# RWKV-7 chain steps in a hybrid decoder layer: first products per head in half-width tiles with one eviction, and the state decayed ahead on GpSimd

## The chip, the cores and the metric

The kernel runs on one core of one Trainium2 chip. The metric is the device time of one execution in microseconds, lower is better. Engine names are those of the profile: PE is TensorE's matmul, PEld its weight load, DVE is VectorE, ACT is ScalarE, POOL is GpSimd, SP is SyncE, which issues most DMAs. Within one engine instructions run in the order in which they were put into its queue.

## The reference, cut to what matters

One layer of a decoder for 512 prompt tokens and 8 short sampled sequences of 8 tokens (576 tokens in all): RMSNorm, one wide projection, two token mixers side by side (a Mamba-2 part and an RWKV-7 part, 16 heads of 64 each), an output projection, a SwiGLU block and a gated per-layer embedding. The change lies in the RWKV-7 part, whose recurrence per token and head is

```python
def step(s, inp):
    r_t, w_t, k_t, v_t, kk_t, a_t = inp
    s_kk = jnp.einsum('bhvk,bhk->bhv', s, kk_t)
    s = (s * w_t[:, :, None, :] - s_kk[..., None] * (kk_t * a_t)[:, :, None, :]
         + v_t[..., None] * k_t[:, :, None, :])
    return s, jnp.einsum('bhvk,bhk->bhv', s, r_t)
```

Everything is computed in float32.

## The kernel before

**Tiling.** The 16 heads are worked in four quarters of four heads: two column groups `jj`, and in each two heads `e`. Head `e` lies in partitions 0 to 63 or 64 to 127, named `H[0]` and `H[1]`. The 576 tokens are nine groups `g` of 64: group 0 holds the sampled tokens, groups 1 to 8 the prompt. The recurrence is evaluated group by group: within a group it is a set of small matrix products with a triangular inverse `TT`, made beforehand by `solve` and `combine` of the quarter; from group to group a state of 64 by 64 per head is carried on.

**One step of the chain** (`core(g)`, then `prompt_state(g)` and `outp(g)`, for g from 1 to 8 in turn, with group 0 put in after group 1) goes through these hops:

1. PE, line 789: for each `jj` one product with 128-column weights `Gt[:, g, jj, 0]` (both heads side by side) and the 128 columns `sv[:, jj, 0]` (state and values of both heads). Of the 2 by 2 blocks of the result the two on the diagonal are used.
2. These blocks are evicted from PSUM into `xs`: the lower partitions by ACT (line 791, recorded under line 93 as `xs<-cx`), the upper ones by DVE (line 792).
3. PE, line 797: the inverse `TT` times `xs`, four products of 64 by 64. Behind them, line 802 begins the outputs.
4. ACT (line 804) and DVE (line 805) evict the negated result into `suv`.
5. PE, line 823: `dw`, what the group adds to the state. PE, line 812, finishes the outputs, and ACT evicts them into `ar`.
6. DVE, lines 827 to 832: four instructions, one per `jj` and head, each old state times its decay `PC` plus `dw`, written into the `suv` tile of the next group (or into `so` after group 8). Hop 1 of the next step reads it.

`bktok` and `vwin` make transposed operands of coming steps; `sampled` handles group 0. The pool tag `suv` has three buffers, `xs` two; PSUM tiles `cx` have two banks.

**What stands around it.** The text calls, for each quarter, the projections that are still missing, `prep`, `start_states`, `gram`, `bonus`, `decayed`, `inverse` and `chain`. But the order of the instructions on each engine is not that of the text: the tile framework plans it while the program is built, from an estimated timeline of all engines (`schedule_with_timeline_sim=True`), so projections and preparation of the next quarter (`lin` products, recorded under lines 221 to 223; their weight splits `whi` on ACT and `wlo` on POOL or DVE, lines 203 and 206; convolutions, line 395; masks of `gram` on POOL, lines 634 and 638; the solve's elimination steps on DVE, lines 674 and 676) lie between the steps of a chain. A few places are fixed by hand: some fillers are issued after marks that `core` leaves (`marks[q, g]`, its last first-product).

Of the kernel before, what the change touches and what calls it, by code (L numbers as in the profile page):

```python
# [8 lines left out]
F32 = mybir.dt.float32  # L9
F32R = mybir.dt.float32r  # L10
AF = mybir.ActivationFunctionType
ALU = mybir.AluOpType
# [4 lines left out]
P = 128  # L17
# [58 lines left out]
def hybrid_step(ctx, tc, A):  # L76
    nc = tc.nc
    V, S, G, T = nc.vector, nc.scalar, nc.gpsimd, nc.tensor
# [9 lines left out]
    def nm(s):  # L88
        uid[0] += 1
        return f"{s}_{uid[0]}"  # L90

    def act(out, in_, func=AF.Copy, scale=1.0, bias=0.0):
        return S.activation(out, in_, func, bias=bias, scale=scale)  # L93

    def root_ready(ins):

        with tc.issue_after(ins.ins):
            t = cp.tile([P, 1], F32, tag="rr", name=nm("rr"), bufs=2)
            act(t[:], eps_t[:, 2:3], AF.Sqrt)
# [7 lines left out]
    def lin_ps(off=224):  # L107
        return lin_bank()[:, off:off + NT]

    def bank(pool, tag, bufs):  # L110
        return pool.tile([P, 512], F32, tag=tag, name=nm(tag), bufs=bufs)
# [138 lines left out]
    sp = mix.enter_context(tc.tile_pool(name="sp", bufs=1, side="right"))  # L250
# [15 lines left out]
    def cx_ps():  # L266
        return bank(sq_, "cx", 2)

    def tr_ps():
        return bank(sq_, "tr", 1)  # L270
# [7 lines left out]
    def cslot(name, shape=None, dt=F32):  # L278
        return sp.tile(shape or [P, NT], dt, tag="cv", name=nm(name), bufs=3)
# [27 lines left out]
    for k in range(KT):  # L307
        sq = (se, sp)[k % 2].tile([P, NT], F32, tag=f"bk{k % 2}", name=nm("sq"), bufs=2)
        e = G if k in SQP else V
# [143 lines left out]
    H = (slice(0, 64), slice(64, 128))  # L453
    jj2 = (0, 1)
# [266 lines left out]
    def load_states(s):  # L721
        t = sp.tile([P, 8, 2, 64], F32, tag="L", name=nm("S0"))
        nc.sync.dma_start(t[:], A["s_wkv"][s.q])
        return t
# [14 lines left out]
    def chain(s):  # L739
        TT = s.TT  # L740
        q, AR, Gt, BK, vv, PC = s.q, s.AR, s.G, s.BK, s.v, s.PC
        SUV = [None] * 9

        def suv(g):
            if SUV[g] is None:
                SUV[g] = sp.tile([P, 2, 2, 2, 64], F32, tag="suv", name=nm("suv"), bufs=3)
            return SUV[g]

        def vput(g, ps, half):
            src = ps[half].rearrange("p (j c) -> p j c", j=2)  # L750
            for e in range(2):
                act(suv(g)[H[1 - e], :, :, e],
                    src[:, :, e * 64:e * 64 + 64].unsqueeze(2).to_broadcast([64, 2, 2, 64]))

        def vwin(g):

            ps = tr_ps()
            a = min(g, 7) * 64
            for jj in jj2:
                T.transpose(ps[:, jj * P:(jj + 1) * P], vv[jj][:, a:a + 128], ident[:])  # L760
            for i in range(g, min(g + 2, 9)):
                vput(i, ps[:, 0:256], H[i - min(g, 7)])

        bkt = {}

        def bktok(g):
            ps = tr_ps()
            for jj in jj2:
                T.transpose(ps[:, jj * P:(jj + 1) * P], BK[jj][:, g].rearrange("p a t -> p (a t)"), ident[:])
            t = sp.tile([P, 2, P], F32, tag="bkt", name=nm("bkt"), bufs=2)  # L770
            act(t[:].rearrange("p a c -> p (a c)"), ps[:, 0:256])
            bkt[g] = t

        outs = {}
        flat = lambda t: t.rearrange("p e t -> p (e t)")

        def pairs(ps):

            return ps[:, 0:256].rearrange("p (j e c) -> p j e c", j=2, e=2)

        def singles(ps):

            return ps[:, 0:128].rearrange("p (j c) -> p j c", j=2)

        def core(g):
            sv = suv(g)
            xw = pairs(cx_ps())
            for jj in jj2:
                marks[q, g] = T.matmul(xw[:, jj], flat(Gt[:, g, jj, 0]), sv[:, jj, 0], start=True, stop=True)
            xs = sp.tile([P, 2, 64], F32, tag="xs", name=nm("xs"), bufs=2)  # L790
            act(xs[H[0]], xw[H[0], :, 0])
            V.tensor_copy(xs[H[1]], xw[H[1], :, 1])
            ups = cx_ps()
            uw = ups[:].rearrange("p (j v) -> p j v", j=8)
            for jj in jj2:
                for e in range(2):
                    T.matmul(uw[H[e], jj, :], TT[H[e], g, jj, :], xs[H[e], jj, :], start=True, stop=True)  # L797
            outs[g] = ow = singles(cx_ps())
            for jj in jj2:
                for e in range(2):  # L800
                    rho = s.Z[H[e], jj, 1, :] if g == 0 else AR[H[e], jj, g]
                    T.matmul(ow[H[e], jj], sv[H[e], jj, 0, e], rho, start=jj == 0, stop=False,
                             skip_group_check=True)
            act(sv[H[0], :, 1, 0], uw[H[0], 0:2, :], scale=-1.0)
            V.tensor_scalar(sv[H[1], :, 1, 1], uw[H[1], 0:2, :], -1.0, None, ALU.mult)

        def outp(g):
            sv = suv(g)
            ow = outs[g]
            for jj in jj2:  # L810
                for e in range(2):
                    T.matmul(ow[H[e], jj], sv[:, jj, 1, e], Gt[:, g, jj, 1, e], start=False, stop=True,
                             skip_group_check=True)
            out = act(AR[:, :, g], ow)
            if q == 3 and g == 8:
                root_ready(out)

        def prompt_state(g):
            sv = suv(g)
            dw = singles(cx_ps())  # L820
            for jj in jj2:
                for e in range(2):
                    T.matmul(dw[H[e], jj], bkt[g][:, jj, e * 64:e * 64 + 64], sv[:, jj, 1, e], start=True, stop=True)
            so = None
            if g == 8:
                so = sp.tile([P, 2, 64], F32, tag="xs", name=nm("so"), bufs=2)
            for jj in jj2:
                for e in range(2):
                    h = H[e]
                    dst = so[h, jj] if g == 8 else suv(g + 1)[h, jj, 0, e]  # L830
                    V.scalar_tensor_tensor(dst, sv[h, jj, 0, e], PC[h, jj, 7 + g:8 + g], dw[h, jj],  # L831
                                           ALU.mult, ALU.add)
            if g == 8:
                nc.sync.dma_start(A["o_wkv_p"][q], so[:])

        def sampled():
            S0 = load_states(s)
            bktok(0)
            core(0)
            outp(0)  # L840
            sv = suv(0)
            for jj in jj2:
                dps = cx_ps()
                ums = [sp.tile([P, 8, 64], F32, tag="gt", name=nm("um"), bufs=2) for _ in range(2)]
                for e, um in enumerate(ums):
                    G.tensor_tensor(um[:], sv[:, jj, 1, e].unsqueeze(1).to_broadcast([P, 8, 64]),
                                    dmb[:].unsqueeze(2).to_broadcast([P, 8, 64]), ALU.mult)
                for e, um in enumerate(ums):
                    T.matmul(dps[H[e], :], bkt[0][:, jj, e * 64:e * 64 + 64], um[:].rearrange("p b v -> p (b v)"),
                             start=True, stop=True)  # L850
                V.tensor_tensor(S0[:, :, jj, :], dps[:].rearrange("p (b v) -> p b v", b=8), S0[:, :, jj, :], ALU.add)
                G.tensor_tensor(S0[:, :, jj, :], S0[:, :, jj, :], PC[:, jj, 0:8].unsqueeze(2).to_broadcast([P, 8, 64]),
                                ALU.mult)
            nc.sync.dma_start(A["o_wkv_s"][q], S0[:])

        for e in range(2):
            G.memset(suv(1)[H[e], :, 0, e], 0.0)
        vwin(0)
        for e in range(2):
            G.tensor_copy(suv(0)[H[e], :, 0, e], ident[H[e], H[e]].unsqueeze(1).to_broadcast([64, 2, 64]))  # L860
        for g in range(1, 9):
            if g == 2:
                vwin(g)
            bktok(g)
            core(g)
            if g % 2 and 1 < g < 8:
                vwin(g + 1)
            prompt_state(g)
            outp(g)
            if g == 1:  # L870
                sampled()

    YR, marks = [], {}
# [382 lines left out]
    for what in SEQ:  # L1256
# [7 lines left out]
        elif what == "y":  # L1264
            for j in range(6):
                t = cslot("yl")
                nc.sync.dma_start(t[:], yr_d[j][:])
                YR.append(split(t[:], xp, ("xhi", "xlo"), [P, NT], lo_eng=G))
        else:
            ps = lin_ps()  # L1270
            linear(YR[0:6], ps)
            t = cslot("pr")
# [21 lines left out]
    for c in range(8):  # L1294
        ps = lin_ps()
# [59 lines left out]
    for f in range(2):  # L1355
        ps = lin_ps()
# [20 lines left out]
    for k in range(4):  # L1377
        xa, xb, t = ft("xa"), ft("xb"), ft("tt")
# [100 lines left out]
    for a, b in ((0, 320), (320, NT)):  # L1479
# [18 lines left out]
        for c in range(8):  # L1498
# [5 lines left out]
            ps = lin_bank()[:, 0:n]  # L1504
# [8 lines left out]
            t = ft("pg")[:, 0:n]  # L1513
# [8 lines left out]
        ps = rstd_by_token(acc, 1.0 / D, 0, n)  # L1522
        rl = ft("rs")[:, 0:n]
        act(rl, ps)
        for c in range(8):
            h = hs[c][:, a:b]
# [146 lines left out]
```

## Time and profile before

| | us |
|---|---|
| median of 3 timed runs | 1347.17 |
| lowest, highest | 1346.14, 1347.79 |
| span of the profiled execution, first to last instruction | 1349.0 |
| first and last chain product of line 789 begin at | 201.3 and 671.4 |

The profile is of one execution on the chip. Its span is 1.8 us above the median of the timed runs. A row of the grouped view gives line, engine, operation, output and inputs, shape and count, then busy microseconds and the mean nanoseconds of one, then the engine's idle time ahead of it and what ended it. A float32 matmul stands as two PE records. The view of waits gives, for a pair of waiting and releasing instruction, total microseconds, times, and the longest. The view of windows gives for each stretch its length, busy time (and instruction count) of PE, PEld, DVE, ACT and POOL, then the clock granted to TensorE (1 is full speed), the DMA share and GB/s. In the timeline a row is start, duration, engine, line, operation, output and inputs, count, and in brackets the idle time before it with its releaser.

### The profile page before, as it was taken

Reading aid. Unit: us, or ns where it says so; the run is one execution under the profiler, and the core shown is the slowest. Engines: PE = TensorE matmul, PEld = TensorE weight load, DVE = VectorE, ACT = ScalarE, POOL = GpSimd, SP = SyncE. Lnnn points to the kernel's source line nnn. Section 1 sums busy time; section 2 is a strip of 40 time slices with the busy share of each in tenths; the row PEclk is TensorE's granted clock in tenths of the full one; section 3 lists DMA queues with packets and bytes.
Section 4 is the critical chain, followed back from the end, with each engine's and each line's share of the span. In section 5 each row is a group of like instructions: output and inputs, shape, how many; then the busy total and the mean of one; then the engine's idle time right before and its main releaser. Section 6 shows DMA issues by size and latency. Waiting matters only on the chain.

```text
span 1349.0 us, 26596 instructions
## 1 busy us (share of the span) xinstructions
PE 1246.8 (92%) x10525; PEld 1150.7 (85%) x10525; DVE 826.0 (61%) x1443; ACT 618.9 (46%) x1256; POOL 625.6 (46%) x597
## 2 busy tenths in 40 slices
PE   6897999999989978899999969989999999999997
PEld 6787897889868957788779859889999999999997
DVE  6648666887687785943466667886553135443454
ACT  6565436534654463343434364464442124433363
POOL 5425413642355154122456645565654336654642
PEclk9897799899979978889989989998999999999998
DMA  5322242234232412262454542222323222314322
GB/s 164 125 68 66 77 117 63 85 103 116 75 99 78 109 41 80 94 214 83 157 176 131 179 125 72 73 93 88 92 88 87 79 86 82 93 59 149 96 89 71
DMA packets 94461, 135.58 MB, mean 100 GB/s; under 512 B 34705, under 2 KB 39057, under 8 KB 94337
## 3 DMA queue, kind: packets, MB, share of 16 engines
q1 hardware_dynamic: 93760, 133.36, 32.4%
q8 instruction: 83, 1.36, 0.4%
q10 hardware_dynamic: 576, 0.52, 0.1%
q14 instruction: 42, 0.34, 0.1%
HBM read 106.10 MB, written 27.75 MB: 99 GB/s over the span
## 4 chain that ended last, share of the span: by engine, by line
PE 63%; DVE 14%; ACT 4%; issue 4%; DMA 3%; POOL 3%; DVEq 0%; SPq 0%; ACTq 0%; POOLq 0%
PE lin L234 21%; PE lin L1403 8%; PE lin L223 6%; PE lin L221 6%; PE lin L222 6%; DVE h L395 2%; PE lin L1508 1%; PE lin L1509 1%; PE lin L1510 1%; DVE tmp L674 1%; DVE wlo L206 1%; DVE Tt L676 1%; PE lin L613 1%; PE cx L797 1%; DVE suv L831 1%
## 5 line engine op out<-in xcount | busy, mean ns | idle before, releaser
L206 POOL TENSOR_TENSOR wlo<-raw,whi 128x512 fp32r<-128x512 f32 (+1 forms) x108 | 146.4, 1356 | 352.5 <-ACT whi L93 269.5
L93 ACT ACTIVATE whi<-raw 128x512 fp32r<-128x512 f32 (+1 forms) x232 | 143.3, 618 | 259.1 <-PE lin L234 126.4
L221 PE MATMUL lin<-xhi,whi 128*128 128x288 f32 (+1 forms) x784 | 243.3, 311 | 2.5 <-ACT whi L93 2.2
L223 PE MATMUL lin<-xhi,wlo 128*128 128x288 f32 (+1 forms) x784 | 241.5, 308 | 2.3 <-POOL wlo L206 2.3
L222 PE MATMUL lin<-xlo,whi 128*128 128x288 f32 (+1 forms) x784 | 241.5, 308 | 0.3 <-POOL xlo L194 0.3
L206 DVE TENSOR_TENSOR wlo<-raw,whi 128x512 fp32r<-128x512 f32 (+1 forms) x124 | 100.9, 814 | 103.2 <-PE lin L234 60.4
L221 PEld LDWEIGHTS lin<-xhi,whi 128*128 128x128 f32 (+1 forms) x784 | 151.0, 193 | 9.3 <-ACT whi L93 2.6
L223 PEld LDWEIGHTS lin<-xhi,wlo 128*128 128x128 f32 (+1 forms) x784 | 150.7, 192 | 6.2 <-POOL wlo L206 2.8
L222 PEld LDWEIGHTS lin<-xlo,whi 128*128 128x128 f32 (+1 forms) x784 | 150.8, 192 | 4.8 <-issue 1.2
L234 PE MATMUL lin<-xhi,whi 128*128 128x288 f32 x384 | 62.3, 297 | 3.2 <-ACT xhi L93 3.0
L234 PE MATMUL lin<-xlo,whi 128*128 128x288 f32 x384 | 60.8, 298 | 0.0
L234 PE MATMUL lin<-xhi,wlo 128*128 128x288 f32 x384 | 59.3, 297 | 0.0
L234 PEld LDWEIGHTS lin<-xhi,whi 128*128 128x128 f32 x384 | 54.6, 189 | 3.8 <-ACT xhi L93 1.7
L234 PEld LDWEIGHTS lin<-xlo,whi 128*128 128x128 f32 x384 | 54.8, 191 | 0.0
L234 PE MATMUL lin<-ah,wlo 128*128 128x288 f32 x352 | 54.7, 296 | 0.0
L234 PE MATMUL lin<-al,whi 128*128 128x288 f32 x352 | 54.7, 296 | 0.0
L234 PE MATMUL lin<-ah,whi 128*128 128x288 f32 x352 | 54.7, 296 | 0.0
L234 PEld LDWEIGHTS lin<-xhi,wlo 128*128 128x128 f32 x384 | 54.3, 191 | 0.0
L1403 PE MATMUL lin<-T,wh 128*128 128x288 f32 x320 | 50.1, 296 | 4.5 <-DVE T L194 2.8
L674 DVE TENSOR_TENSOR tmp<-L,Tt 72x30 f32<-72x30 f32 (+14 forms) x120 | 49.2, 410 | 3.2
L234 PEld LDWEIGHTS lin<-ah,whi 128*128 128x128 f32 x352 | 49.6, 189 | 0.0
L234 PEld LDWEIGHTS lin<-ah,wlo 128*128 128x128 f32 x352 | 49.6, 189 | 0.0
(425 smaller groups left out, 3197.8 us busy)
## 6 DMA issues: line engine op xcount, KB each, us to landing
raw<-wts SPq DMA_DIRECT2D x271, 256.0 KB, 2.6
S<-s_wkv SPq DMA_DIRECT2D x8, 512.0 KB, 5.1
hd<-s_ssm SPq DMA_DIRECT2D x8, 512.0 KB, 4.5
o_ssm_s<-hd SPq DMA_DIRECT2D x8, 512.0 KB, 2.9
xbc_d<-E SPq DMA_DIRECT2D x12, 288.0 KB, 2.1
x<-xT SPq DMA_DIRECT2D x8, 288.0 KB
gate_d<-g SPq DMA_DIRECT2D x8, 288.0 KB, 2.5
bv_d<-rw SPq DMA_DIRECT2D x8, 288.0 KB
```

What stands on the lines that cost most here:

```text
L93: return S.activation(out, in_, func, bias=bias, scale=scale)
L206: eng.tensor_tensor(lo[:, 0:n], raw[:, 0:n], hi[:, 0:n].bitcast(F32), ALU.subtract)
L221: T.matmul(ps[:, a:b], whi, xhi[:, a:b], start=first, stop=False)
L222: T.matmul(ps[:, a:b], whi, xlo[:, a:b], start=False, stop=False)
L223: T.matmul(ps[:, a:b], wlo, xhi[:, a:b], start=False, stop=last)
L234: T.matmul(ps[:, a:e], (hi, lo)[p][:, i * P:(i + 1) * P], xs[k + i][q][:, a:e], start=n == k + i == 0, stop=n == 2 and k + i == nk - 1, sk ...
L395: V.scalar_tensor_tensor(h[:], E[:, i:i + 600], w(i), h[:], ALU.mult, ALU.add)
L613: T.matmul(ps[:, c:c + 128].rearrange("p (a t) -> p a t", a=2), s.BK[jj][H[e], g].rearrange("p a t -> p (a t)"), s.G[H[e], g, jj, :, e], s ...
L674: V.tensor_tensor(o, L[:, jx:jx + 1, jx + 1:32].to_broadcast([NB, jx, n]), Tt[:, 0:jx, jx:jx + 1].to_broadcast([NB, jx, n]), ALU.mult)
L676: V.tensor_tensor(Tt[:, 0:jx, jx + 1:32], Tt[:, 0:jx, jx + 1:32], o, ALU.subtract)
L797: T.matmul(uw[H[e], jj, :], TT[H[e], g, jj, :], xs[H[e], jj, :], start=True, stop=True)
L1403: T.matmul(ps, (hi, lo)[p][:, k * P:(k + 1) * P], OPS[n][k][q], start=first and p == q == k == 0, stop=p == 1 and k == 3, skip_group_check ...
```

## The change

Line 789's products are made per head: 64-column weights, 64 moving columns, into the head's half of the partitions, so that only the used blocks are computed, and they lie side by side as one 128 by 128 block. One ACT instruction evicts them. For groups 1 to 8 a new function `decay(g)` multiplies the state at the beginning of the step with its decay on POOL, one instruction per head for both `jj`, into a new tile `kept` of one buffer; the state's update on DVE is then one addition of `kept` and `dw` per head for both `jj`.

```diff
-        def pairs(ps):
-            return ps[:, 0:256].rearrange("p (j e c) -> p j e c", j=2, e=2)
+        kept = {}
+        def decay(g):
+            kept[g] = t = sp.tile([P, 2, 64], F32, tag="kept", name=nm("kept"))
+            for e in range(2):
+                h = H[e]
+                G.tensor_tensor(t[h], suv(g)[h, :, 0, e], PC[h, :, 7 + g].unsqueeze(2).to_broadcast([64, 2, 64]), ALU.mult)
...
         def core(g):
             sv = suv(g)
-            xw = pairs(cx_ps())
+            xw = singles(cx_ps())
             for jj in jj2:
-                marks[q, g] = T.matmul(xw[:, jj], flat(Gt[:, g, jj, 0]), sv[:, jj, 0], start=True, stop=True)
+                for e in range(2):
+                    marks[q, g] = T.matmul(xw[H[e], jj], Gt[:, g, jj, 0, e], sv[:, jj, 0, e], start=True, stop=True)
             xs = sp.tile([P, 2, 64], F32, tag="xs", name=nm("xs"), bufs=2)
-            act(xs[H[0]], xw[H[0], :, 0])
-            V.tensor_copy(xs[H[1]], xw[H[1], :, 1])
+            act(xs[:], xw)
+            if g:
+                decay(g)
...
-            for jj in jj2:
-                for e in range(2):
-                    h = H[e]
-                    dst = so[h, jj] if g == 8 else suv(g + 1)[h, jj, 0, e]
-                    V.scalar_tensor_tensor(dst, sv[h, jj, 0, e], PC[h, jj, 7 + g:8 + g], dw[h, jj],
-                                           ALU.mult, ALU.add)
+            for e in range(2):
+                h = H[e]
+                dst = so[h] if g == 8 else suv(g + 1)[h, :, 0, e]
+                V.tensor_tensor(dst, kept[g][h], dw[h], ALU.add)
```

More of the change, by code (lines that the diff above doesn't have):

```diff
@@ L774, in chain @@
         outs = {}
-        flat = lambda t: t.rearrange("p e t -> p (e t)")
-        def pairs(ps):
-            return ps[:, 0:256].rearrange("p (j e c) -> p j e c", j=2, e=2)
+        kept = {}
[4 more added lines that the diff above has]
+                G.tensor_tensor(t[h], suv(g)[h, :, 0, e], PC[h, :, 7 + g].unsqueeze(2).to_broadcast([64, 2, 64]), ALU.mult)
         def singles(ps):
```

## The prediction

> **What bounds the kernel now.** I read the page first, then the windows over the four chains, the waits in them, and the timeline of one step.
>
> ```profile
> span 1349.0 us, 26596 instructions
> ...
> PE 1246.8 (92%) x10525; PEld 1150.7 (85%) x10525; DVE 826.0 (61%) x1443; ACT 618.9 (46%) x1256; POOL 625.6 (46%) x597
> ...
> PE 63%; DVE 14%; ACT 4%; issue 4%; DMA 3%; POOL 3%; DVEq 0%; SPq 0%; ACTq 0%; POOLq 0%
> ```
>
> PE is busy nearly always and holds 63% of the chain that ended last; DVE holds 14% of it, POOL 3%. An average over the span says little of one stage, so here are the windows of the four quarters' chains.
>
> ```profile
> 195.00:320.00 125.00, 117.38 (x1127) 102.46 (x1121) 95.52 (x200) 62.57 (x140) 55.50 (x71) 0.93 0.29 87
> 320.00:440.00 120.00, 111.45 (x1091) 98.05 (x1089) 88.39 (x174) 63.08 (x144) 51.36 (x60) 0.90 0.32 94
> 440.00:555.00 115.00, 101.88 (x1046) 85.82 (x1044) 85.38 (x191) 54.86 (x126) 39.65 (x45) 0.91 0.29 82
> 555.00:680.00 125.00, 116.22 (x1063) 96.21 (x1062) 61.96 (x151) 53.51 (x122) 38.34 (x38) 0.90 0.44 142
> sum 485.00, PE 446.94 PEld 382.54 DVE 331.25 ACT 234.02 POOL 184.84; mean PE 111.73 PEld 95.63 DVE 82.81 ACT 58.50 POOL 46.21
> ```
>
> PE is idle for 485.0 - 446.9 = 38 us here, and its granted clock is 0.90 to 0.93, so it is not simply full. DVE is busy for 74 to 76% of the first three windows. Whatever the chain gains must come from these 38 us, from the clock, or from DVE's queue. The waits of this stretch (total us, times, longest):
>
> ```profile
> POOL wlo L206 <- ACT whi L93: 139.5, 23, 19.2
> ...
> DVE suv L805 <- ACT suv L93: 13.1, 10, 4.2
> ...
> PE cx L789 <- DVE suv L831: 6.6, 4, 2.9
> PE cx L797 <- DVE xs L792: 6.3, 4, 2.8
> ...
> PEld cx L789 <- DVE suv L831: 3.8, 5, 3.0
> ```
>
> The two longest that PE spends on the chain are just the two DVE hops that the change touches: the copy of line 792 and the update of line 831. One step shows why (timeline, and one stretch's granted clock):
>
> ```profile
> 271.22 1.21 DVE L831 SCALAR_TENSOR_TENSOR suv<-suv,pc,cx 64x64 f32<-64x64 f32 x4
> 274.26 0.61 PE L789 MATMUL cx<-suv,G 128*128 128x128 f32 x4
> 274.91 0.27 ACT L93 ACTIVATE xs<-cx 64x128 f32<-64x128 f32 x1 [3.31 <-PE cx L789]
> 277.85 0.32 PE L797 MATMUL cx<-xs,TT 64*64 64x64 f32 x2
> 280.50 0.29 DVE L792 COPY xs<-cx 64x128 f32<-64x128 f32 x1
> 280.84 0.38 PE L797 MATMUL cx<-xs,TT 64*64 64x64 f32 x5 [2.34 <-DVE xs L792]
> 284.24 1.29 POOL L206 TENSOR_TENSOR wlo<-raw,whi 128x512 fp32r<-128x512 f32 x1 [6.59 <-ACT whi L93]
> 284.30 1.43 DVE L674 TENSOR_TENSOR tmp<-L,Tt 72x184 f32<-72x184 f32 x1
> 285.76 0.36 DVE L676 TENSOR_TENSOR Tt<-Tt,tmp 72x184 f32<-72x184 f32 x1
> 288.18 1.19 DVE L831 SCALAR_TENSOR_TENSOR suv<-suv,pc,cx 64x64 f32<-64x64 f32 x4
> ```
> ```profile
> 282.40:285.40 3.00, 3.00 (x15) 2.85 (x13) 2.83 (x7) 1.78 (x4) 1.16 (x1) 0.51 0.58 170
> ```
>
> ACT has its half of `xs` at 275.18. DVE, in the middle of the next quarter's elimination, copies its half only at 280.50. PE starts the inverse product with one half and then stands 2.34 us for the other. Just behind that idle time the granted clock is 0.51 for 3 us, so the wait is paid once more at 3.0 x 0.49 = 1.5 us.
>
> **The change part by part.** Durations of what goes and what comes, and the nearest rows for what the trace has not:
>
> ```profile
> L831 DVE SCALAR_TENSOR_TENSOR suv<-suv,pc,cx 64x64 f32<-64x64 f32 x112 | 31.3, 280 | 13.7 <-PE cx L823 11.2
> L792 DVE COPY xs<-cx 64x128 f32<-64x128 f32 x36 | 10.6, 294 | 15.4 <-ACT xs L93 14.8
> L831 DVE SCALAR_TENSOR_TENSOR so<-suv,pc,cx 64x64 f32<-64x64 f32 x16 | 4.5, 280 | 0.9 <-PE cx L823 0.6
> L623 DVE TENSOR_TENSOR Lst<-lin,dgmask 64x128 f32<-64x128 f32 x8 | 2.3, 288 | 0.8 <-ACT G L93 0.7
> ```
> ```profile
> L93 ACT ACTIVATE ar<-cx 128x128 f32<-128x128 f32 x36 | 9.9, 276 | 17.7 <-PE cx L812 17.4
> L93 ACT ACTIVATE xs<-cx 64x128 f32<-64x128 f32 x36 | 9.6, 268 | 24.8 <-PE cx L789 24.5
> ```
> ```profile
> L638 POOL TENSOR_TENSOR G<-G,gmask 64x256 f32<-64x256 f32 x32 | 21.4, 667 | 10.5 <-ACT G L93 8.6
> ...
> L638 POOL TENSOR_TENSOR G<-G,dgmask 64x128 f32<-64x128 f32 x8 | 3.5, 433 | 4.4 <-ACT G L93 4.1
> ...
> L857 POOL MEMSET suv<- 64x128 f32 x8 | 1.6, 201 | 13.9 <-ACT whi L93 7.7 <-DVE suv L831 6.0
> ```
>
> *One eviction.* ACT's grows from 268 to about 276 ns (a 128x128 PSUM block, as the outputs): nothing. DVE loses 36 x 294 = 10.6 us. PE's wait for it, 6.3 us, goes; what is late next is ACT's eviction, which PE waits for anyway. **-6.3 us.** Two of the waits were over 2 us (2.34 and 2.8), long enough for the slow clock: **-3 us**.
>
> *State update.* Four instructions of 280 ns (1.19 us in the step shown) become two of 64x128 with one PSUM input, 288 ns each by the mask row: 0.6 us, so 0.54 us earlier. PE waited for it nine times (6.6 us in 4, 3.8 in 5); each of them shortens by 0.54: **-4.9 us.** The rest of these waits is DVE's queue and stays.
>
> *DVE's load.* Gone: 10.6 + 31.3 + 4.5 = 46.4 us; added: 64 x 288 ns = 18.4 us; net 28.0 us less. DVE stands in the last chain for 14% of the span and is busy for 61%: 0.23 of an average DVE microsecond is paid for. 28.0 x 0.23 = 6.4, of which 4.9 is counted: **-1.5 us**. The bounds are 0 and, where DVE alone set the end, -28.
>
> *POOL.* Two multiplies per step, 64 in all. The trace has none of them; a 64x128 memset (201 ns) bounds one below and a 64x256 mask product (667) above; I take the 64x128 mask product, 433: 64 x 0.433 = 27.7 us. By POOL's share of the chain (3% against 46% busy) that costs 27.7 x 0.065 = **+1.8 us**. Queued behind each pair are `wlo` (PE waits for that), the masks of `gram` and the products `um`; each may come up to 0.87 us later.
>
> POOL's work is not free for DVE either: the elimination product of 72x184 took 1.43 us at 284.30, while `wlo` ran on POOL until 285.53, and the following one of the same size took 0.36. If each of the 64 multiplies met such an instruction, DVE would lose 27.7 us; with DVE busy 68% of the stretch (331 of 485) and a meeting half over on the average I take 27.7 x 0.68 x 0.5 = 9.4 us, at 0.23: **+2.2 us**. The Trainium skill, "SBUF — State Buffer", section "Who interferes with whom", gives a rule that speaks against the change: a VectorE instruction with two SBUF inputs and a GpSimd instruction that reads SBUF exclude each other for a whole instruction. By it, with every multiply meeting one, this term would be 27.7 x 0.23 = 6.4, and the time 4 us longer than my sum; the 1.43 us above agrees with the rule. The new addition on DVE has one SBUF input, and the old one had one too.
>
> *PE.* Between fillers the new shape is no gain:
>
> ```profile
> 286.18 0.29 PE L221 MATMUL lin<-xhi,whi 128*128 128x288 f32 x1
> 286.40 0.45 PE L823 MATMUL cx<-suv,bkt 128*64 128x64 f32 x8
> 286.68 0.40 PE L812 MATMUL cx<-G,suv 128*64 128x64 f32 x6
> 287.02 0.40 PE L222 MATMUL lin<-xlo,whi 128*128 128x288 f32 x1
> ...
> 290.18 0.29 PE L221 MATMUL lin<-xhi,whi 128*128 128x288 f32 x1
> 290.31 0.61 PE L789 MATMUL cx<-suv,G 128*128 128x128 f32 x4
> 290.67 0.38 PE L222 MATMUL lin<-xlo,whi 128*128 128x288 f32 x1
> ```
>
> From filler to filler the old four records take 290.67 - 290.18 = 0.49 us. Half-width products start 0.22 us after a filler, and 14 of them are 0.62 us up to the next; at that rate 8 take 0.22 + 8/14 x 0.62 = 0.57 us: +0.08 a step, or +3 us in 36 steps. Against it, the inverse product is no longer entered twice (277.85 and 280.84 in the step shown); each such second entry costs 0.22 - 0.13 = 0.09 us of changing shape, in 36 steps at most 3 us. I take **0**, with bounds of 3 us to both sides.
>
> **Sum:** -6.3 - 3 - 4.9 - 1.5 + 1.8 + 2.2 = -11.7 us. Against the profiled span that is 1349.0 - 11.7 = 1337.3; the runs' median, 1347.2, lies 1.8 us under the span, so I predict 1335.5, rounded to **1336 us**, 0.8% faster. No DMA is added or moved, and SP's queue is untouched. The planned order of 485 us is made anew from other costs, which no row prices; I allow 7 us to each side for it.
>
> **The rivals.**
>
> *Late multiplies (slower).* The addition on DVE now also waits for POOL. POOL runs in order, and for 139.5 of these 485 us it stands in front of a `wlo` whose `whi` ACT has not made; the mean wait is 6.1 us, the longest 19.2. A multiply queued behind one comes when that wait and 1.3 us of `wlo` are over. The addition then stands on DVE with the elimination, masks and `wlo` behind it, and the next first product with it. Against it: in the step shown the old state is written at 271.22 + 1.21 = 272.43 and the update that needs the product of POOL comes at 288.18, and 36 steps in 485 us are 13.5 us apart on average, so on average only a wait of more than 13.5 - 1.3 - 0.9 = 11.3 us comes through. A late step costs between 0 and 19.2 - 11.3 = 7.9 us, 4 in the middle, plus 1.5 of slow clock: 5.5. Two of them take 11 us of the 11.7, three make it slower, and five, 27.5 us, give 1347.2 - 11.7 + 27.5 = **1363**. Chance 0.20, milder cases included.
>
> *The wait moves on (no change).* Both hops are followed by another DVE eviction of the same step, line 805, waiting 13.1 us already. If DVE's queue, not the number of hops, sets the pace, the 6.3 and 3 us come back there: -11.7 + 9.3 = -2.4, **1345**. For it: the copy at 280.50 was late for its place in the queue, and line 805 has the same queue. Against it: a hop less is a queueing less. Chance 0.15.
>
> *DVE was the bound (more).* If the first three windows hang on DVE, all its 28 us count, less the 9.4 it loses to POOL: 18.6, and with PE's wait and clock 28: **1320**. For it: 75% busy there, with the elimination in one dependent row. Against it: PE is busy 89 to 94%. Chance 0.13.
>
> That the change does not do what it says would need a second eviction or a fourth update; its text leaves none.
>
> **How the numbers follow.** Forecast 0.52 (1336, own range 1328 to 1343), more 0.13, no change 0.15, slower 0.20. About 0.2%, 2.7 us, is what a measurement of this kernel can tell from no change. Faster by more: 0.52 + 0.13 = 0.65; within: 0.15; slower: 0.20. The range must leave out at most 2 in 10: 1322 leaves out about half of the "more" case, 0.07, and 1353 the worse half of the slower one, 0.11.
>
> **What would show it.** Right: no wait of line 797's product for a DVE copy; the update pair under 0.65 us; DVE's busy time some 20 us lower over the four chains, POOL's 28 higher; the clock there up by 0.01; line 789's last product before 671.4. Wrong: DVE additions that wait for POOL's `kept`; waits of line 805's successors grown by what line 797 lost; first products per head that take longer than 0.6 us from filler to filler; multiplies far from 433 ns; or the time after 680 changed, which none of this touches.

## The result, and the profile after

| | median, us (runs) | ratio to before, 95% interval |
|---|---|---|
| before, run beside it | 1343.52 (20) | 1 |
| after | 1347.51 (20) | **1.0028 [1.0015, 1.0040]** |

The change makes the kernel 0.28% slower: 4.0 us between the medians, where 11.7 us less had been forecast. Ratios leave out the few executions that took far longer: one of before (1392.22 us), and below one of eight of `order_both` (3865.70) and two of twelve of `after_null` (1906.70 and 2253.71). The median of before is itself 3.65 us below that of the three runs shown ahead of the prediction. A second profile of before (below: "before, second profile") has a span of 1340.1 us, 8.9 less than the first, and is the one compared with from here on.

The page of after, and its windows over the four chains (columns as in the prediction):

```profile
span 1348.5 us, 26867 instructions
...
PE 1238.7 (92%) x10669; PEld 1141.4 (85%) x10669; DVE 805.1 (60%) x1343; ACT 617.9 (46%) x1256; POOL 662.3 (49%) x661
...
PE 67%; DVE 13%; ACT 4%; DMA 3%; issue 3%; POOL 2%; SPq 0%; DVEq 0%; POOLq 0%; ACTq 0%
...
L783 POOL TENSOR_TENSOR kept<-suv,pc 64x128 f32<-64x128 f32 x64 | 34.3, 536 | 66.6 <-DVE suv L836 54.5
```
```profile
195.00:320.00 125.00, 115.56 (x1134) 100.61 (x1133) 94.05 (x180) 62.24 (x140) 62.47 (x86) 0.92 0.30 86
320.00:440.00 120.00, 105.80 (x1122) 93.09 (x1121) 81.47 (x150) 63.08 (x145) 60.70 (x76) 0.93 0.31 91
440.00:555.00 115.00, 104.07 (x1046) 87.28 (x1046) 77.83 (x162) 54.05 (x124) 46.72 (x57) 0.82 0.28 80
555.00:680.00 125.00, 114.38 (x1123) 93.37 (x1121) 54.97 (x121) 52.82 (x121) 46.03 (x55) 0.92 0.44 142
sum 485.00, PE 439.81 PEld 374.36 DVE 308.32 ACT 232.18 POOL 215.92; mean PE 109.95 PEld 93.59 DVE 77.08 ACT 58.05 POOL 53.98
```

The third window and the sum of before, second profile:

```profile
440.00:555.00 115.00, 101.06 (x1067) 84.86 (x1065) 88.43 (x199) 56.67 (x130) 40.06 (x45) 0.94 0.30 86
sum 485.00, PE 446.52 PEld 380.71 DVE 331.41 ACT 235.27 POOL 188.85; mean PE 111.63 PEld 95.18 DVE 82.85 ACT 58.82 POOL 47.21
```

The loads moved as the change says: over the four windows DVE has 331.4 - 308.3 = 23.1 us less, POOL 215.92 - 188.85 = 27.1 more. But the third window's clock is 0.82 (0.94 in the second profile of before, 0.91 in the first). PE's groups on the chain's hops between 195 and 690 us show where it stands now. Each row ends with PE's idle time ahead of the group and what ended it; first before (second profile), then after:

```profile
L789 PE MATMUL cx<-suv,G 128*128 128x128 f32 x144 | 29.2, 320 | 7.3 <-DVE suv L831 6.9 <-DVE S L851 0.3
L812 PE MATMUL cx<-G,suv 128*64 128x64 f32 x288 | 28.1, 242 | 0.8 <-ACT suv L93 0.4 <-DVE suv L805 0.3
L797 PE MATMUL cx<-xs,TT 64*64 64x64 f32 x288 | 25.1, 245 | 9.7 <-DVE xs L792 6.1 <-DVE S L851 1.6 <-ACT xs L93 1.5
L613 PE MATMUL lin<-G,bk 64*128 64x128 f32 x216 | 25.1, 343 | 1.7 <-ACT E L93 1.2 <-ACT G L93 0.4
L823 PE MATMUL cx<-suv,bkt 128*64 128x64 f32 x256 | 16.5, 248 | 1.0 <-DVE suv L805 1.0
```
```profile
L613 PE MATMUL lin<-G,bk 64*128 64x128 f32 x216 | 29.8, 392 | 8.8 <-POOL bk L585 4.8 <-ACT G L93 3.9
L818 PE MATMUL cx<-G,suv 128*64 128x64 f32 x288 | 29.0, 249 | 0.9 <-ACT suv L93 0.9
L794 PE MATMUL cx<-suv,G 128*64 128x64 f32 x288 | 19.7, 254 | 7.8 <-DVE suv L836 7.8
L803 PE MATMUL cx<-xs,TT 64*64 64x64 f32 x288 | 18.8, 246 | 5.0 <-ACT xs L93 4.8
L829 PE MATMUL cx<-suv,bkt 128*64 128x64 f32 x256 | 17.0, 253 | 7.8 <-DVE suv L811 7.8
```

In after, line 794 is the first products, 803 the inverse, 829 `dw`, 811 the DVE eviction into `suv`, 836 the addition, 783 the multiply. The inverse products stand 5.0 us instead of 9.7, since no DVE copy is waited for. But `dw` stands 7.8 instead of 1.0, and line 613, the next quarter's `gram`, 8.8 instead of 1.7. All hops, that is these groups without line 613 (and with 0.5 us of line 808 in after): 18.8 us before, 22.0 after.

By stretches, each from one event's start in the timeline to the next (the solve's first DVE instruction, the chain's first product, the first product behind the chain), and the same for the experiment that decided the case:

| stretch, us | before, first and second profile | after | change in before's order, two profiles |
|---|---|---|---|
| start to the second quarter's solve | 276.2, 273.7 | 276.1 | 274.1, 275.3 |
| to the third's solve | 142.2, 142.1 | 142.6 | 142.3, 142.6 |
| to the fourth's solve | 118.2, 115.1 | 119.0 | 116.4, 114.4 |
| to the last chain's first product | 59.3, 58.9 | 59.6 | 57.0, 57.0 |
| last chain | 79.2, 79.1 | 77.8 | 79.0, 79.0 |
| to the SwiGLU block | 210.8, 211.3 | 212.2 | 207.9, 210.2 |
| to the end | 463.3, 459.8 | 461.2 | 459.4, 460.9 |

Two executions of one program, before, differ by up to 3.5 us in a stretch. A difference of that size between single profiles can't be put down to an edit.

### The profile page after: what moved, and what is told of

The parts are those of the page before. It is cut to its first block, busy times and chain, and to the rows that moved or that the text cites. A ratio compares the mean times of both kernels' runs of the same rounds, so it can differ in the third digit from the quotient of the medians.

```text
span 1348.5 us, 26867 instructions
## 1 busy us (share of the span) xinstructions
PE 1238.7 (92%) x10669; PEld 1141.4 (85%) x10669; DVE 805.1 (60%) x1343; ACT 617.9 (46%) x1256; POOL 662.3 (49%) x661
## 4 chain that ended last, share of the span: by engine, by line
PE 67%; DVE 13%; ACT 4%; DMA 3%; issue 3%; POOL 2%; SPq 0%; DVEq 0%; POOLq 0%; ACTq 0%
PE lin L234 22%; PE lin L1407 8%; PE lin L221 6%; PE lin L223 6%; PE lin L222 6%; PE lin L613 2%; PE lin L1512 1%; PE lin L1514 1%; PE lin L1513 1%; DVE h L395 1%; DVE wlo L206 1%; PE cx L818 1%; PE tr L769 1%; PE cx L803 1%; DMA L<-Ld 1%
## 5 line engine op out<-in xcount | busy, mean ns | idle before, releaser
L783 POOL TENSOR_TENSOR kept<-suv,pc 64x128 f32<-64x128 f32 x64 | 34.3, 536 | 66.6 <-DVE suv L836 54.5
L613 PE MATMUL lin<-G,bk 64*128 64x128 f32 x288 | 39.3, 394 | 15.1 <-POOL bk L585 9.0
```

Source lines behind the costliest of these rows:

```text
L613: T.matmul(ps[:, c:c + 128].rearrange("p (a t) -> p a t", a=2), s.BK[jj][H[e], g].rearrange("p a t -> p (a t)"), s.G[H[e], g, jj, :, e], s ...
L783: G.tensor_tensor(t[h], suv(g)[h, :, 0, e], PC[h, :, 7 + g].unsqueeze(2).to_broadcast([64, 2, 64]), ALU.mult)
```

## The experiments

Three theories stood after the result. **Plan:** the steps are shorter, but every edit makes the planner draw the order of all engines anew, and that gave the gain back. **Path:** the waits that went were not on the path that sets the end. **GpSimd:** the multiplies stand in POOL's queue ahead of the next quarter's preparation.

### Each half alone, the multiplies on DVE, and a reordered text, all under the planner

`a_only` has the half-width products and the one eviction, `b_only` the decay ahead on POOL; `ab_dve` is the whole change with the multiplies on DVE; `null1` is before with two lines swapped:

```diff
-                G.tensor_tensor(t[h], suv(g)[h, :, 0, e], PC[h, :, 7 + g].unsqueeze(2).to_broadcast([64, 2, 64]), ALU.mult)
+                V.tensor_tensor(t[h], suv(g)[h, :, 0, e], PC[h, :, 7 + g].unsqueeze(2).to_broadcast([64, 2, 64]), ALU.mult)
...
+            V.tensor_copy(xs[H[1]], xw[H[1], :, 1])
             act(xs[H[0]], xw[H[0], :, 0])
-            V.tensor_copy(xs[H[1]], xw[H[1], :, 1])
```

> Only the first half of the change: first products per head in half-width tiles and one ACT eviction; the state's update stays four DVE instructions. Theory 'GpSimd' (the multiplies on POOL delay the preparation of the next quarter, and eat what the chain gains): 0.996 to 0.999 of before, DVE busy over the four chains about 10 us less, POOL unchanged. Theory 'shape' (half-width products between 128-wide fillers cost PE more than they save): 1.002 to 1.004. Theory 'plan' (every edit redraws the planned order, and that alone moves the time by some tenths of a per cent): anything from 0.996 to 1.004, unrelated to the other parts.

> Only the second half: the decay multiplied ahead on POOL and one addition per head on DVE; products and evictions of the first hop as before. 'GpSimd': 1.003 to 1.006, POOL 30 us busier over the four chains, PE waits for POOL's bk in the gram products (5 us or more). 'Shape': 0.996 to 0.999. 'Plan': unrelated to the sum of the parts, so that the two halves' ratios need not multiply to 1.0028.

> The whole change with the two multiplies on DVE in place of POOL (DVE then has 64 more instructions of about 0.3 us, 18 us less relief). 'GpSimd': 0.996 to 1.000, clearly under the whole change's 1.0028. 'Shape': still 1.002 to 1.004. 'Plan': anything.

> The kernel before with the same instructions; only the two evictions into xs are written in the other order in the text, DVE's ahead of ACT's, which the planner takes as its cue. 'GpSimd' and 'shape': within 0.998 to 1.002. 'Plan': may differ by more than 0.2% either way though no work differs.

Measured: `a_only` 1.0031 [1.0007, 1.0055], `b_only` 1.0078 [1.0049, 1.0108], `ab_dve` 1.0021 [0.9998, 1.0043], `null1` 1.0116 [1.0093, 1.0139]. The halves, +0.31% and +0.78%, don't add to the whole's +0.28%, and `ab_dve` is not clearly under the whole change. So neither half, nor POOL, explains the whole's time by itself. `null1` turned out to be no pure reordering. Its waits, and those of before (second profile), in 195 to 690 us:

```profile
ACT xs L93 <- DVE xs L791: 33.9, 18, 5.7
```
```profile
DVE xs L792 <- ACT xs L93: 14.8, 12, 3.4
```

The two evictions wait for each other in the order of the text. With DVE's first, ACT waits for DVE's queue, 33.9 us in 18 times. How much of its 1.16% is this wait and how much the plan is not shown.

### The change in before's order

The planned order of each engine in before is written out as a table, and neighbours in it are tied by edges of issue order, which add no wait to the program. Products, eviction and additions take the places of what they replace; only the multiplies on POOL are left to the planner. `order_a` and `order_b` do the same with each half. Without the change this gives before's program again.

```diff
+def pin_order(nc, tc):
...
+    for engine, steps in plan.items():
+        at, prev = 0, None
+        for d in steps:
+            at += d
+            ins = own[engine][at]
+            if prev is not None:
+                tc.add_manual_dep(ins, prev.name, mybir.DependencyInfo(
+                    mybir.DependencyClass.NoSync, mybir.DependencyReason.DATA), reason="pin")
+            prev = ins
...
             hybrid_step(ctx, tc, A)
+            pin_order(nc, tc)
```

> The whole change, but with the planned order of before written out as edges of issue order (no waits): every instruction that both kernels share stands where it stands in before on its engine; the products, the one eviction and the two additions stand in the places of what they replace, the two POOL multiplies go where the planner likes. It takes the redraw of the order out of the comparison. Theory 'plan' (the steps are shorter as forecast, and the redrawn order gives the gain back): clearly faster than before, 1334 to 1340 us. Theory 'path' (the waits that went were not on the path that sets the end, so that another wait takes their place whatever the order): within 2 us of before. Theory 'GpSimd' (the multiplies stand in POOL's queue in front of the next quarter's preparation): slower than before by 2 to 8 us.

> Half-width products and the one eviction alone, in the planned order of before. With its own order this half took 1.0031 of before. Theory 'plan': 0.993 to 0.998 of before, since the DVE copy (6.3 us of PE waits) is gone. Theory 'shape' (narrow products between wide fillers cost PE more than the copy did): 1.001 to 1.004. Theory 'path': 0.999 to 1.001.

> State decayed ahead on POOL alone, in the planned order of before. With its own order this half took 1.0078 of before. Theory 'plan': 0.996 to 1.000 (the update is shorter by 0.57 us in 28 steps, most of it under fillers). Theory 'GpSimd': 1.003 to 1.008, as with its own order. With 'plan' the two halves add to the whole in this order, which they don't with their own orders (0.31 and 0.78 per cent against 0.28).

> The whole change in before's order once more, beside the next two, and to see whether the gain stands on another chip or another call. Theory 'plan': 0.993 to 0.998 of before again. If the first result was chance: 0.999 to 1.002.

| in before's order | median, us | ratio to before, 95% interval |
|---|---|---|
| whole change, `order_both` | 1337.57 | 0.9954 [0.9926, 0.9981] |
| whole change again, `order_both2` | 1339.49 | 0.9968 [0.9942, 0.9993] |
| half A, `order_a` | 1342.27 | 0.9990 [0.9970, 1.0010] |
| half B, `order_b` | 1343.95 | 0.9998 [0.9980, 1.0016] |

Each ratio is to the executions of before run beside it (medians 1342.59 us, for `order_both2` 1343.76), and is not the quotient of the two medians.

The same instructions that are 0.28% slower in their own order are 0.46 and 0.32% faster in before's; the intervals don't overlap. That decides for **plan**: in a fixed order the change is worth 0.46 and 0.32%, 0.39% of 1343.5 = 5.2 us between them, and the redraw costs (1.0028 - 0.9961) x 1343.5 = 9.0 us (9.9 and 8.1 by the two runs). It is also the fastest version of the study, ahead of both kernels. The halves' -0.10 and -0.02% are each compatible with nothing and, within their intervals, with adding up to the whole. PE's hops in `order_both`:

```profile
L818 PE MATMUL cx<-G,suv 128*64 128x64 f32 x288 | 28.1, 243 | 1.0 <-ACT suv L93 0.4 <-DVE suv L811 0.4
L613 PE MATMUL lin<-G,bk 64*128 64x128 f32 x216 | 26.7, 360 | 1.9 <-ACT E L93 1.2 <-ACT G L93 0.3 <-POOL bk L585 0.2
L803 PE MATMUL cx<-xs,TT 64*64 64x64 f32 x288 | 22.7, 244 | 5.3 <-ACT xs L93 4.5 <-ACT TT L93 0.8
L794 PE MATMUL cx<-suv,G 128*64 128x64 f32 x288 | 20.4, 252 | 4.7 <-DVE suv L836 4.0 <-ACT ar L93 0.4 <-DVE S L855 0.3
L829 PE MATMUL cx<-suv,bkt 128*64 128x64 f32 x256 | 16.9, 252 | 2.3 <-DVE suv L811 2.3
```

The hops stand 13.3 us here (14.5 in `order_both2`) against 18.8 before and 22.0 in after, and line 613 only 1.9 (4.4). So with the order held, 4.3 to 5.5 us of hop waiting go, about what the time gains. That the one is the other is not shown. `order_a` has only 14.6 us of hop waiting too, and gains 0.10%; `null1` has 17.9, less than before, and is 1.16% slower.

Nor do the profiles show where the 5.2 us are gained. The last chain ends at 675.0 and 669.0 us in the two profiles of before, at 668.7 and 668.2 in those of `order_both` and `order_both2`. What the redraw costs does show there, as far as single profiles tell: five profiles of changed kernels in the planner's order (after, `a_only`, `ab_dve`, and `after_null` and `after_null2` below) end the last chain at 674.7 to 676.2, `b_only` at 681.0, and seven with the order held in whole or in part (these four runs and the first three under "Which engines") at 666.8 to 670.9.

What the redraw did can be seen at two places. The first is POOL near 250 us. After (timelines of POOL and PE):

```profile
250.45 1.85 POOL L783 TENSOR_TENSOR kept<-suv,pc 64x128 f32<-64x128 f32 x2 [0.40 <-DVE suv L836]
252.36 0.60 POOL L389 COPY cso<-E 128x3 f32<-128x3 f32 x1
252.91 0.83 POOL L388 COPY cso<-E 128x24 f32<-128x24 f32 x1
253.69 3.29 POOL L585 TENSOR_TENSOR bk<-lo,lo 64x576 f32<-64x576 f32 x2
```
```profile
251.49 0.49 PE L613 MATMUL lin<-G,bk 64*128 64x128 f32 x4
255.14 1.22 PE L613 MATMUL lin<-G,bk 64*128 64x128 f32 x4 [2.54 <-POOL bk L585]
```

The multiplies were put ahead of the `bk` products, and PE has no other work there and stands 2.54 us for `bk`. In before's order:

```profile
253.64 3.35 POOL L585 TENSOR_TENSOR bk<-lo,lo 64x576 f32<-64x576 f32 x2
257.06 1.70 POOL L783 TENSOR_TENSOR kept<-suv,pc 64x128 f32<-64x128 f32 x2
```
```profile
254.26 0.80 PE L613 MATMUL lin<-G,bk 64*128 64x128 f32 x4
256.02 1.22 PE L613 MATMUL lin<-G,bk 64*128 64x128 f32 x4
```

Here the multiplies come behind `bk`. `bk` is no earlier, but PE has other products in front of that place and its rows carry no wait: the order of two engines together makes the wait. The multiplies are not needed for it: in `a_only` and `ab_dve`, which have none on POOL, line 613 stands nearly as long, and for POOL's `bk` too (first `a_only`):

```profile
L613 PE MATMUL lin<-G,bk 64*128 64x128 f32 x216 | 30.9, 403 | 6.2 <-ACT G L93 3.4 <-POOL bk L585 2.8
```
```profile
L613 PE MATMUL lin<-G,bk 64*128 64x128 f32 x216 | 27.5, 365 | 7.2 <-POOL bk L585 4.0 <-ACT G L93 3.0
```

The second place is the third quarter's chain. Windows of after, and the same distance behind the solve's start of before (second profile); the number after POOL's is the clock:

```profile
498.70:508.70 10.00, 6.02 (x58) 3.73 (x56) 6.93 (x10) 4.95 (x12) 6.74 (x7) 0.82 0.35 112
508.70:518.70 10.00, 10.00 (x116) 8.29 (x116) 3.29 (x9) 3.21 (x11) 3.64 (x7) 0.50 0.18 54
518.70:528.70 10.00, 10.00 (x97) 8.60 (x96) 3.84 (x10) 3.60 (x11) 3.50 (x8) 0.50 0.01 2
```
```profile
495.80:505.80 10.00, 7.98 (x47) 3.44 (x45) 7.80 (x10) 4.24 (x10) 9.68 (x7) 1.00 0.21 59
505.80:515.80 10.00, 7.21 (x99) 5.77 (x98) 7.10 (x20) 5.27 (x17) 4.71 (x8) 1.00 0.32 108
515.80:525.80 10.00, 9.03 (x158) 7.48 (x155) 5.62 (x15) 3.95 (x12) 4.92 (x7) 1.00 0.15 22
```

In after PE never stands for 20 us, but at half the clock; before it stands a fifth of the time at full clock. `gram`'s products take 445 ns in 508.7 to 528 of after and 287 in 505.8 to 525.8 of before. It is the stretch to the fourth solve, 3.9 us longer than in the second profile of before, but only 0.9 longer than in the first. That the clock made it longer is argued, not shown: no run changed the clock alone.

### How far the order alone moves the time

`null2` is before with its four state updates in the order of heads. `after_null2` and `after_null` are after with the first products, and with the additions, written upper head first:

```diff
-            for jj in jj2:
-                for e in range(2):
+            for e in range(2):
+                for jj in jj2:
                     h = H[e]
...
-                for e in range(2):
+                for e in (1, 0):
                     marks[q, g] = T.matmul(xw[H[e], jj], Gt[:, g, jj, 0, e], sv[:, jj, 0, e], start=True, stop=True)
...
-            for e in range(2):
+            for e in (1, 0):
                 h = H[e]
                 dst = so[h] if g == 8 else suv(g + 1)[h, :, 0, e]
```

> Before, with the four state updates of a step written head by head instead of column group by column group: the same four instructions, the same operands, nothing else. Only the planner's order can differ. Theory 'plan': it moves the time by several tenths of a per cent either way (the swap of the two evictions moved it by 1.16 per cent); without it 0.999 to 1.001.

> The changed kernel with the four first products of a step written upper head first instead of lower head first, under the planner: the same instructions, only the order can differ. Theory 'plan': another draw, anywhere from 0.995 to 1.010 of before, and off the changed kernel's 1.0028 by more than the intervals. If 1.0028 belongs to the change itself: 1.002 to 1.004.

> The changed kernel with the two additions of a step written upper head first, under the planner; few places move (89 lines of PE's order against 792 between the changed kernel's own order and before's). Theory 'plan': near the changed kernel, 1.001 to 1.005 of before, since the order is nearly its own.

Measured: `null2` 1.0017 [0.9997, 1.0036], `after_null2` 1.0022 [1.0002, 1.0041], `after_null` 0.9991 [0.9966, 1.0017]. `null2` is a pure reordering, and its interval takes in no change at all: redrawing before's own instructions moves the time less than I expected. But none of the three orders that the planner made for the changed instructions (1.0028, 1.0022, 0.9991) is as fast by its ratio as before's order (0.9954, 0.9968), and `after_null` and `after_null2` show the same stands on `dw` (7.9 and 6.8 us) and on line 613 (8.3 and 6.2). So the loss is not in one draw alone. It is not equal in all either: `after_null` is no slower than before, and its interval overlaps those of before's order. Three orders are too few to tell how the planner's orders spread.

### Which engines, and POOL once more

`order_pe` holds PE alone to before's order, `order_rest` (with the four other names in the same place) DVE, ACT, POOL and SP; `order_both_dve` holds all, with the multiplies on DVE.

```diff
     for engine, steps in plan.items():
+        if engine not in ('PE',):
+            continue
```

> The whole change with PE's order alone held to that of before; the planner orders DVE, ACT, POOL and SP anew round it. Theory 'plan, on PE' (what the redraw costs is where the fillers stand on PE between the hops): as fast as with all engines held, 0.993 to 0.998. Theory 'plan, on the side engines' (the order of preparation on DVE, POOL and ACT makes the next quarter's solve late): 1.000 to 1.004, as the change with its own order.

> The whole change with DVE, ACT, POOL and SP held to before's order and PE left to the planner. With PE alone held the gain was gone (1.0004), with all held it was there (0.9954, 0.9968). Theory 'side engines': as all held, 0.994 to 0.998. Theory 'both': 0.999 to 1.003.

> The whole change in before's order, with the two multiplies of a step on DVE instead of POOL. Theory 'GpSimd' (head-of-line waiting of the multiplies in POOL's queue costs time): faster than the whole change in that order by 2 us or more. Theory 'POOL is cover': the same within 2 us, or slower by the 64 multiplies that DVE then carries in the solve's stretches.

> Before unchanged, for a profile of an execution near its median: the profiled one lay at 1349.0 us between first and last instruction, with the clock at 0.89 in the first 195 us where every later profile of any kernel has 0.93. Expected: a span of 1338 to 1344 us, the clock at 0.93 there, and the same stages up to that shift.

Measured: `order_pe` 1.0004 [0.9979, 1.0030], `order_rest` 0.9973 [0.9954, 0.9992], `order_both_dve` 0.9987 [0.9962, 1.0013]. The gain survives when the side engines are held and not clearly when PE is; their intervals still overlap, so this points to the side engines and doesn't settle it. Off POOL, the multiplies make nothing faster, as 0.9987 against 0.9954 and 0.9968 shows: **GpSimd** falls as a cause by itself. Where the planner puts the multiplies in POOL's queue, as near 250 us, belongs to the plan. `before_again`, the second profile, ran once, in 1341.79 us, with a span of 1340.1 as expected. Its stages were not the first profile's up to a shift, as expected: the stretch to the fourth solve took 115.1 us against 118.2.

### What a hop is worth

`order_slow` is before, in its order, with one more link in every step:

```diff
             V.tensor_copy(xs[H[1]], xw[H[1], :, 1])
+            xc = sp.tile([P, 2, 64], F32, tag="xc", name=nm("xc"), bufs=2)
+            V.tensor_copy(xc[:], xs[:])
...
-                    T.matmul(uw[H[e], jj, :], TT[H[e], g, jj, :], xs[H[e], jj, :], start=True, stop=True)
+                    T.matmul(uw[H[e], jj, :], TT[H[e], g, jj, :], xc[H[e], jj, :], start=True, stop=True)
```

> Before, in before's order, with one more link in every step: after the two evictions DVE copies xs (128x128) into a second tile, and the inverse products read that one. It prices a hop: 36 links of about 0.4 us each (an estimate from the DVE copy of 64x128, 0.28 us, and the distance between two instructions on DVE). Theory 'cover' (fillers on PE hide a hop but for the few steps where PE stands, as the waits of before show: some ten of 36): 3 to 8 us slower. Theory 'every hop counts': 12 to 18 us slower. Theory 'path' (the chain's hops don't reach the end at all): within 2 us.

Measured: 1.0083 [1.0054, 1.0113], 11.2 us slower, above "cover" and just under "every hop". Its rows of PE and of the copy, 195 to 690 us:

```profile
L799 PE MATMUL cx<-xc,TT 64*64 64x64 f32 x288 | 22.7, 248 | 28.5 <-DVE xc L794 25.1 <-ACT TT L93 3.3
```
```profile
L794 DVE COPY xc<-xs 128x128 f32<-128x128 f32 x36 | 17.1, 476 | 1.2
```

The inverse products stand 28.5 us instead of 9.7, while the first products behind them stand 2.9 instead of 7.3; over all hops it is 33.3 instead of 18.8. So 14.5 us more waiting came with 11.2 us more time (7.3 to 15.2 by the interval), about three quarters. The copy also puts 17.1 us of work on DVE, so not all of it need be the wait. **Path** falls for a longer hop: it does reach the end, and here it shows in the stages too, as the last chain ends at 685.3 us. That a shorter hop pays at the same rate is not shown.

## Why the prediction was wrong

The forecast was 1336 us, 0.8% faster; the time is 1347.5, inside the range and on the other side. Point by point:

**The step that failed is the last of the sum: "The planned order of 485 us is made anew from other costs, which no row prices; I allow 7 us to each side for it."** It was given no sign and stood outside the sum, as if the two sides were equally likely. It cost 9.0 us, more than the rest was worth, and none of the three orders drawn for the changed instructions was a clear gain.

**One eviction, -6.3.** The wait for the copy went as told. But "what is late next is ACT's eviction, which PE waits for anyway" took ACT's wait as unchanged. With the order held it grew from 1.5 to 4.5 us, and the inverse products' wait fell by 9.7 - 5.3 = 4.4 (3.3 in `order_both2`). The half alone gained 0.10%, 1.3 us, not clear of nothing.

**Slow clock, -3.** Did not come. In before's order the four windows' clock is 0.92, 0.89, 0.91, 0.92 against 0.93, 0.90, 0.94, 0.92 of the second profile. This term had been read off one step and carried to a sum.

**State update, -4.9.** The additions take 285 ns (288 forecast). "PE waited for it nine times" was misread. Four are PE's own waits; the other five are of the weight load (PEld), and one of these is the same wait again (first profile):

```profile
562.58 1.22 PE L789 MATMUL cx<-suv,G 128*128 128x128 f32 x4 [2.85 <-DVE suv L831]
```
```profile
562.57 0.93 PEld L789 LDWEIGHTS cx<-suv,G 128*128 128x128 f32 x4 [2.99 <-DVE suv L831]
```

The remaining four weight loads waited 0.17 to 0.26 us each, with no wait of PE's. So the term is 4 x 0.54 = 2.2 us; the 2.7 too many would have gone to the next term, which takes 6.4 less what is counted here, and the sum stays. With the order held the first products' wait fell from 7.3 to 4.7, by 2.6 (2.1 in `order_both2`), and `dw` gained 1.3 of waiting.

**DVE's load, -1.5.** DVE's whole busy time fell from 825.7 (second profile) to 802.3 us in `order_both`, 23.4 instead of 28.0. The stretch from the fourth solve to the last chain is 1.9 us shorter in both profiles with the order held, near the 1.5. But it is 58.9 to 59.0 in `order_a`, `order_b` and `order_rest`, and DVE carries nearly as little in the last, so that DVE's load made it is not shown.

**POOL, +1.8, and the lock, +2.2.** The multiplies took 34.3 us instead of 27.7, a mean of 536 ns. What they cost on POOL was not measured by itself; moved to DVE they were no cheaper.

**PE, 0.** The products' own price was not measured apart from the eviction.

**Rivals.** "Late multiplies" did not happen: no addition of line 836 is shown waiting for `kept`. It is POOL that waits, 54.5 us for the state. "The wait moves on" happened just as described, from the copy to line 805's eviction (now 811), but mainly in the redrawn order: `dw` stands 7.8 us there, 2.3 with the order held. "DVE was the bound" fell: 23.4 us less on DVE came with 5.2 us less in all.

**The base.** The sum stood on the median of three runs, 1347.2; that of 20 is 1343.5. From it the forecast would have been 1331.8, further off.

So with the order held the change is faster, as forecast, but by 5.2 us where 11.7 were forecast, which lies outside the intervals of both runs (up to 0.74%, 9.9 us). The slow clock's 3 us did not come, and the wait for `xs` fell by 4.4 instead of 6.3. That the 5.2 us come from the hops, as the prediction had it, stays open. The redraw took them back, and 4 us more.

## What to carry to other kernels

Where a planner orders the engines, an edit is two changes, the instructions and the order of everything else: hold the old order to measure the first, and don't take an improved step for an improved kernel. When a late releaser is taken away, price the next one at how late it becomes, not at what it costs now. A hop made longer cost about three quarters of the waiting that it added, in one run, and the sum of hop waits did not rank the kernels, so a sum of waits is not yet a forecast. And profile an unchanged kernel twice before reading single stretches: here they differed by up to 3.5 us.

## What was not expected of the hardware

The clock stayed at 0.50 for 19.3 us in after (508.7 to 528.0) while PE was never idle; in that time no product was wider than 128 columns, and none was a 128x288 filler. The two largest groups:

```profile
L613 PE MATMUL lin<-G,bk 64*128 64x128 f32 x58 | 8.7, 445 | 0.0
L734 PE MATMUL cb<-G,S 64*64 64x16 f32 x64 | 4.2, 266 | 0.0
```

The Trainium skill, "TensorE: Matmul & The Clock Gate", section "Part 1: The HAM clock gate (the "warmup" mystery)", says that full clock comes after about 3.4 us of sustained work. This trace disagrees: five times that, back to back by the profile, did not bring it. In `a_only`, `after_null` and `after_null2` PE is never idle for 12 to 20 us of the same stage, with the clock at 0.50 too. Whether the narrow shapes are the reason was not tried.
